# Two runs of high and low parts in the up products, and high parts first in the down units, of a hybrid encoder layer

## The chip, the cores and the metric

The kernel runs on one core of a Trainium2 chip. The metric is device time in microseconds of one execution, the median of several runs. Times of single instructions come from one profiled execution.

## What is computed

One encoder layer for 512 tokens of width 2048: a projection into a convolution group and an attention group, an output projection with a residual, and then a gated MLP with a width-3 convolution between its up-projection and its activation. The change is in the MLP:

```python
xn = rms_norm(x, ffn_norm_g[l])
up = jnp.einsum("bsd,df->bsf", xn, w_up[l])          # 2048 -> 2 x 5632
up = depthwise_conv(up, ffn_dw_w[l], ffn_dw_b[l])
gate, val = jnp.split(up, 2, axis=-1)
x = x + jnp.einsum("bsf,fd->bsd", jax.nn.silu(gate) * val, w_down[l])
return rms_norm(x, final_norm_g)
```

All inputs and outputs are float32.

## The kernel before, in words

**High and low parts.** Every product runs in the type float32r on TensorE. To keep float32's accuracy, each operand is split: its high part is a float32r copy that ScalarE makes (`whi`, L117), its low part the difference, which VectorE makes (`wlo`, L121). Of the four partial products three are kept: high by high, high by low, low by high (`mm3`, L128 to L136).

**The weights.** `plan` lists, in the order of use, a function for every weight unit of 128 x 1024; `weights()` (L158) hands out the next one and has made the three behind it by then (`AHEAD` is 3). A unit comes in by a DMA on SyncE's queue into one of seven raw buffers, and is split by `parts` (L114) into rings of four high and four low buffers (`NW` is 4). A buffer is written again when the unit four places back is no longer read.

**The up products.** The hidden width is done in 44 tiles f of 128, in chunks of four (`CH` is 4). In each f the gate tile and the value tile, each 2048 by 512 tokens, come from seven smaller products instead of eight, by Strassen's scheme in Winograd's form: seven sums of the weights' quarters (`factors`, L687) times seven sums of the activations' quarters (`comb`, made once at L652). Of each product c there are eight blocks. The activation block `comb[c][k]` holds its high part for 256 columns and its low part for the next 256, so one *wide* matmul of 512 columns with the weight's high part (L773) gives high by high in the left half of a bank and high by low in the right half. A *narrow* matmul of 256 columns (L779) with the weight's low part adds low by high into the right half. ScalarE and VectorE read both halves afterwards, add them, and combine the seven results (L814 to L846).

`up` (L764) does the products in pairs (0, 1), (2, 3), (4, 5), and 6 by itself. In a pair: eight wides of the first, one wide of the second, eight narrows of the first, eight narrows of the second, seven wides of the second. Product 6: seven wides, eight narrows, one wide. The tiles f = 0 and f = 3 go through `up_apart`, with 256 columns only.

**The banks.** `product_bank` (L754) gives the PSUM bank. From the second chunk on products 0 to 5 take turns in the three `mm` banks, and product 6 has the one bank `po`. The two `tr` banks belong to the down units there.

**The down units.** While chunk c is made, chunk c - 1 is multiplied into the output: behind products 3 and 6 of every f stands one down unit (`down_units`, L732; in the last chunk fewer). `down` (L915) takes one weight unit for two output tiles d; for each it does `mm3` over the four hidden tiles k: high by high, high by low, low by high, four times over, 12 wide matmuls in one `tr` bank. ScalarE copies the bank out (L926), and GpSimd's queue adds it to the sum in DRAM (L927). With `wide=True` the same function does the last units at the end, in `mm` and `tr` banks.

**The order.** A scheduler places every engine's instructions from the program's order and the buffers' dependences; within a queue all go in order. Before the change it put some matmuls of a down unit between the products in two f of most chunks. The function `tick` issues side work (statistics of the norm) behind a product; it has none left in the stretch that the change touches.

Of the kernel before, what the change touches and what calls it, by code (L numbers as in the profile page):

```python
# [10 lines left out]
F32 = mybir.dt.float32  # L11
# [5 lines left out]
P = 128  # L17
D = 2048
S = 512
# [15 lines left out]
U = 8  # L35
# [7 lines left out]
CH = 4  # L43
# [23 lines left out]
def layer(ctx: ExitStack, tc: tile.TileContext, xT, xG, xw, w_a, w_in, w_v, w_out, w_up, w_down, par, tab, g3, out, last_out):  # L67
    nc = tc.nc
# [5 lines left out]
    psm = ctx.enter_context(tc.tile_pool(name="psm", bufs=3, space=bass.MemoryType.PSUM))  # L74
    psa = ctx.enter_context(tc.tile_pool(name="psa", bufs=1, space=bass.MemoryType.PSUM))
# [9 lines left out]
    def t2(name, dt=F32):  # L85
        return tp.tile([P, S], dt, tag="t2k", name=name)
# [41 lines left out]
    def mm3(ps, w, wk, mh, ml, start, stop):  # L128
        hi, lo = w[:2]
        a = slice(wk * P, (wk + 1) * P)  # L130
        m = nc.tensor.matmul(ps, hi[:, a], mh, start=start, stop=False)  # L131
        if turned:
            turned.pop()
            pin(m)
        nc.tensor.matmul(ps, hi[:, a], ml, start=False, stop=False)  # L135
        return nc.tensor.matmul(ps, lo[:, a], mh, start=False, stop=stop)  # L136
# [4 lines left out]
    def tick(behind, mid=False):  # L141

        for todo in (steps, asteps):
            while todo and mid == (todo is asteps and amid[0]):
                try:
                    with tc.issue_after(behind.ins):
                        at = next(todo[0])
                    if todo is asteps:
                        amid[0] = at == "mid"
                    break  # L150
                except StopIteration:
                    todo.pop(0)
# [3 lines left out]
    plan, made = [], []  # L156

    def weights():  # L158
        at = weights.at
        weights.at += 1  # L160
        while len(made) < min(at + 1 + AHEAD, len(plan)):
            made.append(plan[len(made)]())
        return made[at]
# [78 lines left out]
    ps = psa.tile([P, 2, S], F32, tag="sc", name="idle")  # L242
# [3 lines left out]
    for k in range(KD):  # L246
        if k < CH:
            raw = t4([P, U * P], "raw")
            n = S + 2 * P + (0 if k else KD)
# [3 lines left out]
        else:  # L253
            if k % CH == 0:
                raw = t4([P, U * P], "raw")
            if k % CH == 0 or k == CH + 2:
                o, n = 2 * (k % CH) * P, 2 * (2 if k < 2 * CH else CH) * P
# [22 lines left out]
    for step in ORDER:  # L280
# [5 lines left out]
        i = next(a_ if step == "a" else q_)  # L286
# [280 lines left out]
    p, n = -1, 0  # L567
# [186 lines left out]
    def product_bank(f, c):  # L754

        n = 7 * f + c
        at = n % 6 if f < CH else 3 * (c == 6)
        if at < 3:
            return psm.tile([P, S], F32, tag="mm", name="pu")
        if at == 3:  # L760
            return psa.tile([P, S], F32, tag="po", name="pu")
        return psa.tile([P, S], F32, tag="tr", name="pu", bufs=2)

    def up(f, between):  # L764

        opened = {}

        def bank(c):
            return product_bank(f, c)

        def wides(c, w, ps, ks, stop=False):
            for k in ks:
                i = nc.tensor.matmul(ps, w[0][:, k * P:(k + 1) * P], comb[c][k], start=k == 0,  # L773
                                     stop=stop and k == ks[-1])
            return i

        def lows(c, w, ps, stop=False):
            for k in range(U):
                i = nc.tensor.matmul(ps[:, H:], w[1][:, k * P:(k + 1) * P], comb[c][k][:, :H], start=False,  # L779
                                     stop=stop and k == U - 1)  # L780
            return i

        def product(c):

            w = weights()
            if c == 6:
                ps = bank(c)
                wides(c, w, ps, range(U - 1))
                lows(c, w, ps)
                i = wides(c, w, ps, range(U - 1, U), stop=True)  # L790
            elif c % 2:
                ps = opened.pop(c)
                lows(c, w, ps)
                i = wides(c, w, ps, range(1, U), stop=True)
            else:
                ps, opened[c + 1] = bank(c), bank(c + 1)
                wides(c, w, ps, range(U))
                wides(c + 1, made[weights.at], opened[c + 1], range(1))
                i = lows(c, w, ps, stop=True)
            tick(i)  # L800
            between(c)
            return ps[:, :H], ps[:, H:]

        def copy(to, ps):
            nc.scalar.activation(to, ps, AF.Copy)  # L805

        def pair(name):
            return t2(name).rearrange("p (i t) -> p i t", i=2)

        def both(x):  # L810
            return x.unsqueeze(1).broadcast_to([P, 2, H])


        vv, low = pair("vv"), pair("pl")  # L814
        for i in range(2):
            m, l = product(i)
            copy(vv[:, i], m)
            copy(low[:, i], l)
        m7, l = product(2)
        add(vv, vv, low)  # L820
        low = pair("pl")
        copy(low[:, 0], l)
        m1, l = product(3)
        copy(low[:, 1], l)
        uu, v = pair("uu"), pair("vl")
        u, u2 = uu[:, 0], uu[:, 1]
        add(u2, m7, low[:, 0])
        add(v, vv, both(u2))
        m6, l = product(4)
        add(u, m1, low[:, 1])  # L830
        low = pair("pl")
        copy(low[:, 0], l)
        add(u2, u, m6)
        m2, l = product(5)
        add(u2, u2, low[:, 0])
        add(v, v, both(u2))
        add(vv[:, 1], vv[:, 1], u2)
        low, g = pair("pl"), pair("g")
        copy(low[:, 0], l)
        add(g[:, 0], u, m2)  # L840
        m3, l = product(6)
        copy(low[:, 1], l)
        add(g[:, 1], vv[:, 1], m3)
        add(g, g, low)
        g, v = (t.rearrange("p i t -> p (i t)") for t in (g, v))
        return g, v  # L846

    def up_apart(f, between):

        def begin(c):  # L850
            return weights(), product_bank(f, c)[:, :H]
# [46 lines left out]
    def hidden(f, between):  # L898
        return gated_tile(f, *(up_apart if f == CH - 1 else up)(f, between))
# [9 lines left out]
    def in_two(g):  # L909
        h, l = t2("hh", F32R), t2("hl", F32R)  # L910
        nc.scalar.activation(h, g, AF.Copy)
        nc.vector.tensor_sub(l, g, h.bitcast(F32))  # L912
        return h, l

    def down(hs, ds, wide=False):  # L915

        for d0 in ds:
            w = weights()
            for d in range(d0, d0 + U // CH):

                ps = (psm.tile([P, S], F32, tag="mm", name="pd") if wide and d % 5 > 1 else
                      psa.tile([P, S], F32, tag="tr", name="pd", bufs=2))
                for k in range(CH):
                    mm3(ps, w, (d - d0) * CH + k, *hs[k], k == 0, k == CH - 1)
                t = t2("pdc")
                nc.scalar.activation(t, ps, AF.Copy)  # L926
                nc.gpsimd.dma_start(xd[d], t, accum_op=ALU.add)  # L927
# [3 lines left out]
    def behind(c, i, at):  # L931
        if c == NCH - 1 and (i, at) == (0, 3):
            pend[-1] = in_two(pend[-1])
        down(pend, down_units(c, i, at))
# [6 lines left out]
    for c in range(NCH):  # L941
        hs = []
        for i in range(CH):
# [5 lines left out]
            if c and i == CH - 1:  # L949
                hs = [in_two(h) for h in hs]  # L950
            hs.append(hidden(c * CH + i, lambda at: None if last else meanwhile(c, i, at)))
        if c != NCH - 2:
            hs = [h if isinstance(h, tuple) else in_two(h) for h in hs]
# [4 lines left out]
    n = CH  # L958
# [17 lines left out]
    for d in down_units(NCH - 1, CH - 1, 6):  # L976
        down(pend, (d,), wide=True)
        last_weights(len(ws))
        last_weights(len(ws))
# [26 lines left out]
    for d in range(KD):  # L1006
        ps = psm.tile([P, S], F32, tag="mm", name="pd")[:, fm]
        for k in range(n):
            mm3(ps, ws[d // CH * CH + k], d % CH, hs[k][0][:, fm], hs[k][1][:, fm], k == 0, k == n - 1)
        i = nc.vector.tensor_add(x2[d][:, fm], x2[d][:, fm], ps)  # L1010
# [7 lines left out]
    wide = psa.tile([P, 2, S], F32, tag="sc", name="pt")  # L1018
    banks = [psa.tile([P, S], F32, tag="tr", name="pt", bufs=2) if g % 2 else wide[:, g // 2] for g in range(CH)]
    rb, xg = [], []  # L1020
    sums, v, r, y, w = (sm.tile([P, CH], F32, tag="rs" + c, name="rs" + c) for c in "lvryw")
    v, r, y, w = (t[:, :1] for t in (v, r, y, w))
# [12 lines left out]
    for g, ps in enumerate(banks):  # L1035
# [5 lines left out]
        for k in range(n):  # L1041
# [3 lines left out]
            i = nc.tensor.matmul(ps, hh[:, tm], dh, start=False, stop=False)  # L1045
# [104 lines left out]
```

## Time and profile before

| | |
|---|---|
| median of 3 runs | 2016.16 us (2015.9 to 2017.13) |
| the profiled execution | 2016.15 us |
| its span, first to last instruction | 2014.4 us |
| granted clock of TensorE, mean | 0.998 |
| up products, and the down units between them | 661.7 to 1937.3 us of the span |
| VectorE busy in that stretch | 1086.41 us |
| ScalarE busy in that stretch | 711.35 us |
| DMA in that stretch | 142 GB/s, engines busy for 0.60 of the time |

A profile line of a group has the source line, the engine, the operation, output and inputs with their shapes, the count, then busy time and mean duration in ns, then the idle time of the engine ahead of it and what ended that. A timeline line has the start and the duration in us; neighbours of one kind are merged (x9), and a bracket tells how long the engine stood idle and who released it. PE is TensorE's matmuls, PEld its weight loads, DVE is VectorE, ACT is ScalarE, POOL is GpSimd, SP is SyncE.

### The profile page before, as it was taken

The page shows a single profiled execution, that of the slowest core. Times are in us where ns is not written, and L with a number is a line of the kernel's source. Part 1 is how long each engine was busy: PE and PEld are TensorE (multiplying, and loading weights), DVE is VectorE, ACT ScalarE, POOL GpSimd, SP SyncE. Part 2 cuts the span into 40 slices and gives each one's busy share as a digit, 9 for nine tenths or more (in the row PEclk, how much of TensorE's full clock was granted, in tenths as well). Part 3 has the DMA queues.
Part 4 walks back from the last instruction along what each step waited for, and adds up shares of the span by engine and source line. Part 5 has one row for each costly group of instructions (what it writes and reads, how often), then busy time and mean ns, then how long its engine had stood idle before and what let it go on. Part 6 is the DMA issues. An engine that isn't in the chain of part 4 may idle for free.

```text
span 2014.4 us, 28027 instructions
## 1 busy us (share of the span) xinstructions
PE 2004.4 (100%) x10510; PEld 1715.7 (85%) x10510; DVE 1667.9 (83%) x2264; ACT 1054.7 (52%) x1689; POOL 169.4 (8%) x201
## 2 busy tenths in 40 slices
PE   9999999999999999999999999999999999999998
PEld 8888888888888998888888888888888888888887
DVE  7996888987576898887888888888888888889875
ACT  6323344476355665555555554555555555555563
POOL 0000000000002101111111111111111111110111
PEclk9999999999999999999999999999999999999999
DMA  7233333346348766556556556555565566564573
GB/s 258 84 106 93 113 95 107 105 139 211 100 136 213 189 163 152 139 129 152 133 135 148 131 131 154 132 139 141 127 145 145 127 145 147 131 141 128 145 206 129
DMA packets 98567, 284.25 MB, mean 141 GB/s; under 512 B 11008, under 2 KB 11520, under 8 KB 98432
## 3 DMA queue, kind: packets, MB, share of 16 engines
q1 hardware_dynamic: 71712, 231.07, 37.4%
q0 software_dynamic: 26720, 51.40, 17.1%
q8 instruction: 83, 1.36, 0.3%
q14 instruction: 52, 0.43, 0.1%
HBM read 227.90 MB, written 54.53 MB: 140 GB/s over the span
## 4 chain that ended last, share of the span: by engine, by line
PE 99%; DMA 0%; ACT 0%; DVE 0%; ACTq 0%; issue 0%; DVEq 0%
PE pu L773 27%; PE pu L779 14%; PE pd L136 8%; PE pd L131 8%; PE pd L135 8%; PE pj L131 6%; PE pj L135 6%; PE pj L136 6%; PE po L131 3%; PE po L135 3%; PE po L136 3%; PE pv L342 1%; PE pv L341 1%; PE pv L340 1%; PE po L535 1%; PE trp L518 1%
## 5 line engine op out<-in xcount | busy, mean ns | idle before, releaser
L117 ACT ACTIVATE whi<-raw 128x1024 fp32r<-128x1024 f32 x364 | 384.5, 1058 | 480.4 <-PE pj L135 131.7
L121 DVE TENSOR_TENSOR wlo<-raw,whi 128x1024 fp32r<-128x1024 f32 x364 | 444.5, 1222 | 208.5 <-ACT whi L117 198.0
L773 PE MATMUL pu<-xc,whi 128*128 128x512 f32 x2352 | 580.0, 391 | 0.0
L773 PEld LDWEIGHTS pu<-xc,whi 128*128 128x128 f32 x2352 | 433.5, 188 | 83.0
L779 PEld LDWEIGHTS pu<-xc,wlo 128*128 128x128 f32 x2352 | 306.8, 191 | 14.6
L779 PE MATMUL pu<-xc,wlo 128*128 128x256 f32 x2352 | 311.3, 283 | 0.0
L136 PE MATMUL pd<-hh,wlo 128*128 128x512 f32 x640 | 250.3, 391 | 0.0
L131 PE MATMUL pd<-hh,whi 128*128 128x512 f32 x640 | 249.7, 390 | 0.0
L135 PE MATMUL pd<-hl,whi 128*128 128x512 f32 x640 | 249.1, 390 | 0.0
L927 POOL DMA_DIRECT2D x2d<-pdc x160 | 138.9, 870 | 1099.0 <-ACT pdc L926 870.1
L131 PE MATMUL pj<-xh,whi 128*128 128x512 f32 x512 | 198.3, 392 | 0.1
L136 PE MATMUL pj<-xh,wlo 128*128 128x512 f32 x512 | 198.2, 390 | 0.0
L135 PE MATMUL pj<-xl,whi 128*128 128x512 f32 x512 | 198.2, 390 | 0.0
L805 ACT ACTIVATE pl<-pu 128x256 f32<-128x256 f32 x294 | 109.9, 382 | 150.1 <-PE pu L773 142.8
L117 ACT ACTIVATE whi<-ws 128x1024 fp32r<-128x1024 f32 x132 | 139.7, 1058 | 72.6 <-PE pu L773 54.2
L396 DVE SCALAR_TENSOR_TENSOR y<-ch,prm,y 128x501 f32<-128x501 f32 (+14 forms) x240 | 173.5, 740 | 4.4
L121 DVE TENSOR_TENSOR wlo<-ws,whi 128x1024 fp32r<-128x1024 f32 x132 | 161.2, 1221 | 14.8 <-ACT whi L117 14.8
L136 PEld LDWEIGHTS pd<-hh,wlo 128*128 128x128 f32 x640 | 120.1, 188 | 28.5 <-DVE wlo L121 3.3
L135 PEld LDWEIGHTS pd<-hl,whi 128*128 128x128 f32 x640 | 120.2, 188 | 25.0 <-DVE hl L912 0.4
L131 PEld LDWEIGHTS pd<-hh,whi 128*128 128x128 f32 x640 | 120.4, 188 | 22.6
L926 ACT ACTIVATE pdc<-pd 128x512 f32<-128x512 f32 x160 | 93.8, 588 | 79.1 <-PE pd L136 66.0
L131 PEld LDWEIGHTS pj<-xh,whi 128*128 128x128 f32 x512 | 96.0, 188 | 20.7 <-ACT g L276 0.3
(228 smaller groups left out, 2721.1 us busy)
## 6 DMA issues: line engine op xcount, KB each, us to landing
raw<-in_w_up SPq DMA_DIRECT2D x176, 512.0 KB, 3.9
raw<-in_w_down SPq DMA_DIRECT2D x88, 512.0 KB, 4.0
x2d<-pdc POOLq DMA_DIRECT2D x160, 256.0 KB, 4.8
raw<-in_w_in SPq DMA_DIRECT2D x60, 512.0 KB, 3.7
raw<-in_w_out SPq DMA_DIRECT2D x32, 512.0 KB, 3.6
raw<-in_w_v SPq DMA_DIRECT2D x16, 512.0 KB, 4.2
tab<-in_tab SPq DMA_DIRECT2D x32, 256.0 KB, 4.9
x<-in_xT SPq DMA_DIRECT2D x16, 256.0 KB, 6.1
```

Of the source, the lines that this page charges most:

```text
L117: i = nc.scalar.activation(hi[:, :n], raw[:, :n], AF.Copy)
L121: j = nc.vector.tensor_sub(lo[:, :n], raw[:, :n], hi[:, :n].bitcast(F32))
L131: m = nc.tensor.matmul(ps, hi[:, a], mh, start=start, stop=False)
L135: nc.tensor.matmul(ps, hi[:, a], ml, start=False, stop=False)
L136: return nc.tensor.matmul(ps, lo[:, a], mh, start=False, stop=stop)
L340: nc.tensor.matmul(ps, xh, wh[:, f], start=kk == 0, stop=False)
L396: nc.vector.scalar_tensor_tensor(y[:, a:b], h[:, a + j - PAD:b + j - PAD], prm[:, o + j:o + j + 1], y[:, a:b], op0=ALU.mult, op1=ALU.add)
L773: i = nc.tensor.matmul(ps, w[0][:, k * P:(k + 1) * P], comb[c][k], start=k == 0, stop=stop and k == ks[-1])
L779: i = nc.tensor.matmul(ps[:, H:], w[1][:, k * P:(k + 1) * P], comb[c][k][:, :H], start=False, stop=stop and k == U - 1)
L805: nc.scalar.activation(to, ps, AF.Copy)
L926: nc.scalar.activation(t, ps, AF.Copy)
L927: nc.gpsimd.dma_start(xd[d], t, accum_op=ALU.add)
```

## The change

From the second chunk on (f of 4 or more), `up` has two runs in place of the pairs: products 0 to 3, then 4 to 6. At the first product of a run, the banks of all of the run are taken, and the wides of all are issued (of the last product only the first); then come the narrows of each product in turn, and behind the narrows of the last one its other seven wides. So a run of four is 25 wides, 32 narrows, 7 wides; a run of three is 17 wides, 24 narrows, 7 wides. The wides of a run use weight units that `weights()` has already made, up to three ahead. For this, `product_bank` gives product 3 the bank `po` as well, which product 6 has; products 0, 1, 2, 4, 5 take turns in the three `mm` banks.

A down unit that isn't `wide` takes both its banks first, then for both output tiles the eight matmuls with the weight's high part (16 in all), then for each tile the four with the low part, its copy and its accumulating DMA. The number of matmuls, copies and DMAs is the same. The first chunk and the units at the end are as before.

```diff
     def product_bank(f, c):
         n = 7 * f + c
-        at = n % 6 if f < CH else 3 * (c == 6)
+        at = n % 6 if f < CH else 3 * (c % 3 == 0 and c > 0)
...
     def up(f, between):
         opened = {}
+        runs = ((0, 1), (2, 3), (4, 5), (6,)) if f < CH else ((0, 1, 2, 3), (4, 5, 6))
...
         def product(c):
             w = weights()
-            if c == 6:
+            run = next(r for r in runs if c in r)
+            if len(run) == 1:
                 ps = bank(c)
                 wides(c, w, ps, range(U - 1))
                 lows(c, w, ps)
                 i = wides(c, w, ps, range(U - 1, U), stop=True)
-            elif c % 2:
+            elif c == run[-1]:
                 ps = opened.pop(c)
                 lows(c, w, ps)
                 i = wides(c, w, ps, range(1, U), stop=True)
             else:
-                ps, opened[c + 1] = bank(c), bank(c + 1)
-                wides(c, w, ps, range(U))
-                wides(c + 1, made[weights.at], opened[c + 1], range(1))
+                if c == run[0]:
+                    for j in run:
+                        opened[j] = bank(j)
+                        wides(j, w if j == c else made[weights.at + j - c - 1], opened[j],
+                              range(1 if j == run[-1] else U))
+                ps = opened.pop(c)
                 i = lows(c, w, ps, stop=True)
...
     def down(hs, ds, wide=False):
+        def bank(d):
+            return (psm.tile([P, S], F32, tag="mm", name="pd") if wide and d % 5 > 1 else
+                    psa.tile([P, S], F32, tag="tr", name="pd", bufs=2))
         for d0 in ds:
             w = weights()
-            for d in range(d0, d0 + U // CH):
-                ps = (psm.tile([P, S], F32, tag="mm", name="pd") if wide and d % 5 > 1 else
-                      psa.tile([P, S], F32, tag="tr", name="pd", bufs=2))
+            two = range(d0, d0 + U // CH)
+            banks = [] if wide else [bank(d) for d in two]
+            for ps, d in zip(banks, two):
                 for k in range(CH):
-                    mm3(ps, w, (d - d0) * CH + k, *hs[k], k == 0, k == CH - 1)
+                    a = slice(((d - d0) * CH + k) * P, ((d - d0) * CH + k + 1) * P)
+                    for i, x in enumerate(hs[k]):
+                        nc.tensor.matmul(ps, w[0][:, a], x, start=k + i == 0, stop=False)
+            for d in two:
+                if wide:
+                    ps = bank(d)
+                    for k in range(CH):
+                        mm3(ps, w, (d - d0) * CH + k, *hs[k], k == 0, k == CH - 1)
+                else:
+                    ps = banks[d - d0]
+                    for k in range(CH):
+                        a = slice(((d - d0) * CH + k) * P, ((d - d0) * CH + k + 1) * P)
+                        nc.tensor.matmul(ps, w[1][:, a], hs[k][0], start=False, stop=k == CH - 1)
                 t = t2("pdc")
                 nc.scalar.activation(t, ps, AF.Copy)
                 nc.gpsimd.dma_start(xd[d], t, accum_op=ALU.add)
```

## The prediction, made before the changed kernel was run

> **What bounds the kernel now.** I read the page first: busy time, granted clock, the chain that ended last.
>
> ```profile
> span 2014.4 us, 28027 instructions
> ...
> PE 2004.4 (100%) x10510; PEld 1715.7 (85%) x10510; DVE 1667.9 (83%) x2264; ACT 1054.7 (52%) x1689; POOL 169.4 (8%) x201
> ...
> PE 99%; DMA 0%; ACT 0%; DVE 0%; ACTq 0%; issue 0%; DVEq 0%
> ...
> L117 ACT ACTIVATE whi<-raw 128x1024 fp32r<-128x1024 f32 x364 | 384.5, 1058 | 480.4 <-PE pj L135 131.7
> ...
> L805 ACT ACTIVATE pl<-pu 128x256 f32<-128x256 f32 x294 | 109.9, 382 | 150.1 <-PE pu L773 142.8
> ```
>
> TensorE is busy for 2004.4 of 2014.4 us, and 99% of the chain is TensorE. The change removes no matmul. So the only time to be had in the gated-MLP stretch is what its matmuls lose against their own steady pitch, and the first question is how much that is. I take it from the stretch between the first and the last up product (windows view, then the groups by shape inside it, then the timeline of one f, TensorE alone).
>
> ```profile
> 661.70:1937.30 1275.60, 1275.60 (x6868) 1105.38 (x6867) 1086.41 (x1383) 711.35 (x1104) 138.00 (x159) 1.00 0.60 142
> ```
>
> ```profile
> L779 PE MATMUL pu<-xc,wlo 128*128 128x256 f32 x2352 | 311.3, 283 | 0.0
> ...
> L135 PE MATMUL pu<-xc,whi 128*128 128x256 f32 x112 | 31.7, 283 | 0.0
> L136 PE MATMUL pu<-xc,wlo 128*128 128x256 f32 x112 | 31.7, 283 | 0.0
> L131 PE MATMUL pu<-xc,whi 128*128 128x256 f32 x112 | 31.7, 283 | 0.0
> ```
>
> ```profile
> 1198.03 2.20 PE L773 MATMUL pu<-xc,whi 128*128 128x512 f32 x9
> 1200.07 2.08 PE L779 MATMUL pu<-xc,wlo 128*128 128x256 f32 x16
> 1201.99 3.59 PE L773 MATMUL pu<-xc,whi 128*128 128x512 f32 x15
> 1205.41 1.12 PE L779 MATMUL pu<-xc,wlo 128*128 128x256 f32 x8
> 1206.37 0.40 PE L131 MATMUL pd<-hh,whi 128*128 128x512 f32 x1
> 1206.60 0.40 PE L135 MATMUL pd<-hl,whi 128*128 128x512 f32 x1
> 1206.84 0.39 PE L131 MATMUL pd<-hh,whi 128*128 128x512 f32 x1
> 1207.16 0.50 PE L136 MATMUL pd<-hh,wlo 128*128 128x512 f32 x1
> 1207.50 0.40 PE L131 MATMUL pd<-hh,whi 128*128 128x512 f32 x1
> ...
> 1209.14 0.39 PE L773 MATMUL pu<-xc,whi 128*128 128x512 f32 x1
> 1209.36 1.11 PE L779 MATMUL pu<-xc,wlo 128*128 128x256 f32 x8
> 1210.31 1.78 PE L773 MATMUL pu<-xc,whi 128*128 128x512 f32 x7
> 1211.93 0.39 PE L135 MATMUL pd<-hl,whi 128*128 128x512 f32 x1
> ...
> 1214.87 2.20 PE L773 MATMUL pu<-xc,whi 128*128 128x512 f32 x9
> 1216.91 2.08 PE L779 MATMUL pu<-xc,wlo 128*128 128x256 f32 x16
> 1218.83 3.36 PE L773 MATMUL pu<-xc,whi 128*128 128x512 f32 x14
> 1222.03 1.12 PE L779 MATMUL pu<-xc,wlo 128*128 128x256 f32 x8
> ```
>
> Matmuls overlap, so their cost is the distance between starts, not the duration. A wide one (512 columns) costs (1200.07 - 1198.03)/9 = 0.2267 us, a narrow one (256) (1201.99 - 1200.07)/16 = 0.120 us. The stretch holds 2352 + 3 x 112 = 2688 narrow ones and 6868 - 2688 = 4180 wide ones: 4180 x 0.2267 + 2688 x 0.120 = 947.6 + 322.6 = 1270.2 us. It lasts 1275.6. So **5.4 us in all** are lost, and no re-ordering can win more than about that (0.27%), unless it changes the pitch itself. Two losses can be seen in the rows, and the change touches both.
>
> **The change part by part.**
>
> *Waits in the down unit.* At 1206.84 to 1207.50 two wide pitches are 0.32 and 0.34 us: 0.66 against 2 x 0.2267 = 0.453, so 0.21 us lost. The waits view of the weight loader names the cause and the count, and VectorE's timeline the time:
>
> ```profile
> PEld pd L136 <- DVE wlo L121: 3.3, 9, 0.4
> ```
>
> ```profile
> 1205.28 0.69 DVE L906 TENSOR_TENSOR uy<-uy 128x512 f32<-128x512 f32 x1
> 1205.88 1.22 DVE L121 TENSOR_TENSOR wlo<-raw,whi 128x1024 fp32r<-128x1024 f32 x1
> ...
> 1213.23 1.23 DVE L121 TENSOR_TENSOR wlo<-ws,whi 128x1024 fp32r<-128x1024 f32 x1 [0.38 <-ACT whi L117]
> 1214.37 0.42 DVE L827 TENSOR_TENSOR uu<-pu,pl 128x256 f32<-128x256 f32 x1
> 1215.99 1.23 DVE L121 TENSOR_TENSOR wlo<-raw,whi 128x1024 fp32r<-128x1024 f32 x1 [1.20 <-ACT whi L117]
> 1217.13 0.69 DVE L828 TENSOR_TENSOR vl<-vv,uu 128x512 f32<-128x512 f32 x1
> 1217.73 0.42 DVE L830 TENSOR_TENSOR uu<-pu,pl 128x256 f32<-128x256 f32 x1
> 1218.14 1.23 DVE L121 TENSOR_TENSOR wlo<-raw,whi 128x1024 fp32r<-128x1024 f32 x1
> ```
>
> The unit's low part ends at 1205.88 + 1.22 = 1207.10, and its first user wants to start at about 1207.07 with its weights already loaded. This happens nine times, once a chunk, in the last f, where VectorE also splits three gated tiles: 9 x 0.21 = 1.9 us. After the change the unit takes 16 wides first (3.63 us), and it stands behind four whole products instead of three: it starts 25 x 0.2267 + 32 x 0.120 + 7 x 0.2267 = 11.1 us into the f instead of 1206.37 - 1198.03 = 8.3. Its first low part is wanted at 1198.03 + 14.7 = 1212.8, 5.7 us behind 1207.10. I take the whole **1.9 us** as gained; between 0, if VectorE's new order makes the low part that much later, and 1.9.
>
> *Wides behind narrows.* Wides that follow wides keep 0.2267. Those that follow narrows do not: 15 took 1205.41 - 1201.99 = 3.42 (15 x 0.2267 = 3.40), 14 took 3.20 (3.174), 7 took 1.62 (1.587): 0.02 to 0.033 us over, and more wides do not add to it, so it is paid once for each stretch of narrows, not per matmul. What is left of the 5.4 us says the same: 5.4 - 1.9 = 3.5. In TensorE's program order I count 189 stretches of narrows before (f 4 to 43: four each, one more in two f of nine chunks, and 11 in the first chunk) and 91 after (two each, and the same 11): 3.5/189 = 0.019 us each. I take 0.020, nearest to the count, and 98 x 0.020 = **2.0 us** gained; the bounds are 0, if it is not the switch that costs, and 98 x 0.033 = 3.2.
>
> [...]
>
> *What is wanted earlier.* A run of four wants its high parts within 25 wides. Within an f, product 1 is wanted where it was (after 8 wides, 1.81 us). Product 2 came after 16 wides and 16 narrows (5.55 us) and comes after 16 wides (3.63); product 3 likewise moves from 7.36 to 5.44, or further where it stood inside the down unit; product 6 from 5.55 to 3.63 us behind the first down unit; its low part from 7.1 to 5.8. Products 4 and 5, and all other low parts, are wanted when they were, or later. ScalarE's timeline shows how far ahead the copies of products 2, 3 and 6 of this f are:
>
> ```profile
> 1192.77 1.06 ACT L117 ACTIVATE whi<-raw 128x1024 fp32r<-128x1024 f32 x1 [1.44 <-PE pu L773]
> ...
> 1198.01 1.06 ACT L117 ACTIVATE whi<-raw 128x1024 fp32r<-128x1024 f32 x1 [1.90 <-PE pd L135]
> ...
> 1212.13 1.07 ACT L117 ACTIVATE whi<-ws 128x1024 fp32r<-128x1024 f32 x1 [3.57 <-PE pu L773]
> ```
>
> They end at 1193.8, 1199.1 and 1213.2, and the new order wants them at 1198.03 + 3.6 = 1201.7, + 5.4 = 1203.5 and + 20.2 = 1218.2: 7.9, 4.4 and 5.0 us ahead. The low part of product 6 ends at 1213.23 + 1.23 = 1214.5 and is wanted at 22.3, so at 1220.3. The ring of four high parts is used up by one run; the buffer for product 3 is the one of the down unit before, and is free 8 lows (1.81 us) before the f starts, 7.2 us before it is wanted, against a copy of 1.06. Cost 0, covered by these leads; if a lead is gone, each us late costs 40 us, once an f.
>
> *Banks and evictions.* Four products now end within 4.5 us and are read by six copies of 0.382 us, 2.3 us of ScalarE. Products 4 and 5 take the banks of 0 and 1, which end 6.6 and 7.6 us into the f and are wanted at 16.5: nothing waits, and where the last chunk has no down unit between, they are still wanted 4.5 us later. A down unit holds both its banks from the start; their last copies are from a unit 11 us back or more. The two results of a unit leave 0.9 us apart instead of 2.7, for ScalarE, then GpSimd's queue, with the same number of DMAs; SyncE's loads move with the raw buffers that the low parts free, and land with the same leads. Cost 0 for all of it; a gain is excluded, since TensorE waited for none of these.
>
> *The sum.* The profiled execution took 2016.15 us, 1.75 more than its span, and the median shown is 2016.16, the same. 2016.15 - 1.9 - 2.0 = **2012.3 us**, a span of 2010.5; 0.19% less.
>
> **The rivals.**
> 1. *The switch costs nothing*, and the 3.5 us belong to something that the order doesn't touch (the rounding of the two pitches alone moves that sum by about 1 us). Against: the three stretches, all over, and in proportion to no count of wides. Only the waits go: 2016.15 - 1.9 = 2014.3. [...]
> 2. *The switch costs what the single stretches show*: 98 x 0.033 = 3.2, with the waits 5.1: 2011.0. For it: the 7 wides at 1210.31. Against: 189 x 0.033 = 6.2 would be more than was lost.
> 3. *Slower: the bank that products 3 and 6 share.* Before, only product 6 used it; now product 6 can't open until VectorE has read product 3, and in VectorE's new order that read stands behind the low part of the second down unit, which needs the first one's buffer, free only at that unit's end. So: unit's end, a low part (1217.13 - 1215.99 = 1.14), two adds that read product 3 and its neighbour (0.41 and 0.42): 1.97 us, against 16 wides = 3.63 until product 6 opens. It decides from 1.66 us more on VectorE at that place. One more low part ahead of it (1.14) still costs nothing; two (2.28) cost 0.6 us, in each of the 36 f with two down units: 22 us, 2034, and 0.22 us an f is enough to be slower by 0.2%. Against: VectorE is 85% busy here (1086 of 1275.6) and has 0.38 and 1.20 us of idle time at just these places above.
> 4. *It doesn't do what it says*: a wait returns behind the new highs. The order as built shows the two runs in every f from 4 on and the highs first in every narrow down unit, so only a late buffer could do this; 1 to 2 us of waits, about 2014.
>
> **How the numbers follow.** Forecast 0.60, over 2011.6 to 2013.2; rival 1 0.14, rival 2 0.12, rival 3 0.08, rival 4 0.06. A measurement of this kernel tells 0.2% from no change, 4.0 us: below 2012.1 is faster, above 2020.2 slower. Faster: rival 2 and two fifths of the forecast, 0.12 + 0.24 = 0.36. Slower: most of rival 3, 0.06. Within: 0.58. For 8 in 10 the range leaves out rival 3 and the far ends: 2010.8 to 2014.4.
>
> **What would show it.** The loader's wait for the low part in the down unit is gone; the same stretch lasts 1271.7 us; behind 32 or 24 narrows the 7 wides again take about 1.62 us, not more, and narrows stay at 0.120; TensorE shows no new wait at product 6's first high. A stretch of 1273.7 with those waits gone is rival 1. A wait for VectorE at product 6 is rival 3. It is wrong altogether if 32 narrows in a row run slower than 0.120, or if the leads of ScalarE's copies, 4.4 us at the least, are eaten by its new order.

## The result, and the profile after

| | before | after |
|---|---|---|
| median, with its runs on the same chips | 2016.77 us (14 runs, 2015.90 to 2017.85) | 2012.70 us (14 runs, 2011.88 to 2013.73) |
| profiled execution | 2016.15 us | 2013.73 us |
| its span | 2014.4 us | 2011.8 us |
| first up matmul's start to the last one's start | 1275.22 us | 1272.78 us |

The ratio is 0.998, with an interval of 0.9973 to 0.9986: the changed kernel is faster by 0.14 to 0.27%. The forecast was 2012.3. The profiled execution of the changed kernel is the slowest of its 14, by 1.0 us over their median, and one place below accounts for that much.

In the changed kernel L774 are the wide up matmuls, L780 the narrow ones, L934 the down unit's high parts and L944 its low parts. The page of the changed kernel:

```profile
span 2011.8 us, 28094 instructions
...
PE 2001.2 (99%) x10510; PEld 1716.8 (85%) x10510; DVE 1659.2 (82%) x2264; ACT 1065.7 (53%) x1689; POOL 171.1 (9%) x201
...
PE 97%; DMA 1%; DVE 0%; ACT 0%; issue 0%; ACTq 0%; POOL 0%; POOLq 0%; DVEq 0%; SPq 0%
```

The work is the same (10510 matmuls, 2264 operations on VectorE), and TensorE is still the chain. The windows view over the up stretch, as for before (start and end, length, then busy time and count of PE, PEld, DVE, ACT, POOL, granted clock, DMA share, GB/s):

```profile
661.80:1934.90 1273.10, 1272.26 (x6868) 1106.54 (x6868) 1076.77 (x1381) 722.21 (x1104) 139.67 (x159) 1.00 0.58 142
```

The same 6868 matmuls at the same clock take 1273.1 us where they took 1275.6; TensorE idles for 0.84 of them. Now the loader's waits, the view that gave the first term. The columns after the arrow are total us, times, longest:

```profile
PEld st L194 <- DVE nl L190: 0.9, 1, 0.9
...
PEld pu L774 <- issue: 0.2, 1, 0.2
```

The line for the down unit's low part (3.3 us, nine times) is gone. New are `st <- nl` (with an `st <- nh` of 0.5 us beside it) and one small wait at an up product. TensorE's timeline of the f that the prediction read:

```profile
1198.04 5.83 PE L774 MATMUL pu<-xc,whi 128*128 128x512 f32 x25
1203.71 4.00 PE L780 MATMUL pu<-xc,wlo 128*128 128x256 f32 x32
1207.54 1.78 PE L774 MATMUL pu<-xc,whi 128*128 128x512 f32 x7
1209.16 0.39 PE L934 MATMUL pd<-hh,whi 128*128 128x512 f32 x1
...
1212.78 1.98 PE L944 MATMUL pd<-hh,wlo 128*128 128x512 f32 x8
1214.60 4.01 PE L774 MATMUL pu<-xc,whi 128*128 128x512 f32 x17
1218.45 3.04 PE L780 MATMUL pu<-xc,wlo 128*128 128x256 f32 x24
1221.32 1.78 PE L774 MATMUL pu<-xc,whi 128*128 128x512 f32 x7
```

Take the distances between starts: 25 wides 5.67 (25 x 0.2267 = 5.67), 32 narrows 3.83 (32 x 0.120 = 3.84), the 7 wides behind them 1.62 against 1.587, 16 wides of the down unit 3.62 (3.627), its 8 low parts 1.82 (1.814). Only the 7 wides behind the narrows lose, 0.033 us, as they did behind 8 narrows before. Narrows win back some 0.01 (3.83 for 3.84, and 24 in 2.87 for 2.88). These rows are rounded to 0.01 us; on the mean of all such places in the two traces the seven wides lose 0.027 us, behind 8, 16, 24 and 32 narrows alike, and the narrows win back about 0.006.

The new wait lies in the first chunk, which the change doesn't touch. VectorE, then TensorE, at 676 us of the changed kernel:

```profile
675.24 0.69 DVE L684 TENSOR_TENSOR acc<-acc,sq 128x512 f32<-128x512 f32 x1 [1.96 <-DMA sq<-sq]
...
676.98 0.68 DVE L190 TENSOR_TENSOR nl<-acc,nh 128x512 fp32r<-128x512 f32 x1
```

```profile
676.11 0.28 PE L136 MATMUL pu<-xc,wlo 128*128 128x256 f32 x1
676.65 0.49 PE L194 MATMUL st<-nh,ones 128*128 128x512 f32 x1 [0.26 <-ACT nh L189]
677.72 0.50 PE L194 MATMUL st<-nl,ones 128*128 128x512 f32 x1 [0.58 <-DVE nl L190]
```

The sum of squares for the norm comes back from DRAM; VectorE waits 1.96 us for it, and the two matmuls of the statistics, which stand in the middle of TensorE's queue, start 0.42 and 0.85 us late, and the next one 0.11: 1.38 us in all. In the profiled execution of before, the same addition ran at 673.10 with no wait. Of the ten traces of this study (before, after and eight experiments) five show such a stand, of 0.4 to 1.4 us, and five show none, though only one edit (of the statistics, below) touches the order of the first chunk. So it belongs to the execution, not to the change.

The account is then: 1275.22 - 1272.78 = 2.44 us shorter as profiled; without the 1.38 of the stand, **3.8 us**, where the prediction had 3.9. The medians are 4.07 apart.

### The profile page after: what moved, and what is told of

It reads as the page before. It is cut to its first block, busy times and chain, and to the rows that moved or that the text cites. A ratio compares the mean times of both kernels' runs of the same rounds, so it can differ in the third digit from the quotient of the medians.

```text
span 2011.8 us, 28094 instructions
## 1 busy us (share of the span) xinstructions
PE 2001.2 (99%) x10510; PEld 1716.8 (85%) x10510; DVE 1659.2 (82%) x2264; ACT 1065.7 (53%) x1689; POOL 171.1 (9%) x201
## 4 chain that ended last, share of the span: by engine, by line
PE 97%; DMA 1%; DVE 0%; ACT 0%; issue 0%; ACTq 0%; POOL 0%; POOLq 0%; DVEq 0%; SPq 0%
PE pu L774 27%; PE pu L780 14%; PE pd L934 14%; PE pd L944 7%; PE pj L131 6%; PE pj L135 6%; PE pj L136 6%; PE po L131 3%; PE po L135 3%; PE po L136 3%; PE pv L341 1%; PE pv L340 1%; PE pv L342 1%; PE pd L136 1%; PE pd L135 1%; PE pd L131 1%
## 5 line engine op out<-in xcount | busy, mean ns | idle before, releaser
L774 PE MATMUL pu<-xc,whi 128*128 128x512 f32 x2352 | 562.8, 390 | 0.0
L774 PEld LDWEIGHTS pu<-xc,whi 128*128 128x128 f32 x2352 | 435.9, 188 | 87.0 <-issue 0.2
L780 PEld LDWEIGHTS pu<-xc,wlo 128*128 128x128 f32 x2352 | 293.9, 192 | 6.8
L780 PE MATMUL pu<-xc,wlo 128*128 128x256 f32 x2352 | 296.1, 283 | 0.0
L934 PE MATMUL pd<-hl,whi 128*128 128x512 f32 x608 | 236.5, 389 | 0.0
L934 PE MATMUL pd<-hh,whi 128*128 128x512 f32 x608 | 236.5, 389 | 0.0
L944 PE MATMUL pd<-hh,wlo 128*128 128x512 f32 x608 | 150.1, 389 | 0.0
L934 PEld LDWEIGHTS pd<-hl,whi 128*128 128x128 f32 x608 | 114.1, 188 | 23.8 <-DVE hl L917 0.2
L944 PEld LDWEIGHTS pd<-hh,wlo 128*128 128x128 f32 x608 | 114.1, 188 | 23.7
L934 PEld LDWEIGHTS pd<-hh,whi 128*128 128x128 f32 x608 | 114.1, 188 | 23.6
L136 PEld LDWEIGHTS pj<-xh,wlo 128*128 128x128 f32 x512 | 96.1, 188 | 20.5
```

What stands on the lines that cost most here:

```text
L934: nc.tensor.matmul(ps, w[0][:, a], x, start=k + i == 0, stop=False)
L944: nc.tensor.matmul(ps, w[1][:, a], hs[k][0], start=False, stop=k == CH - 1)
```

## The experiments

All are variants of the changed kernel unless the text says otherwise. "Stretch" means from the first up matmul's start to the last one's start.

**Each part of the change alone.** The first keeps the runs and puts the old `down` back:

```diff
-            banks = [] if wide else [bank(d) for d in two]
-            for ps, d in zip(banks, two):
-                ...
+            for d in range(d0, d0 + U // CH):
+                ...
+                    mm3(ps, w, (d - d0) * CH + k, *hs[k], k == 0, k == CH - 1)
```

> The two runs of the up products as after, the down unit as before (high, high, low, per block). 92 stretches of narrows against 91 after and 189 before. Theory (each stretch costs 0.02 us, and the down unit's wait goes because the unit stands 2.8 us later in the f): both terms are won by the runs alone, 2012.7 to 2013, and the weight loader's wait for the low part in the down unit is gone. Rival (the wait goes because the unit takes its high parts first): the nine waits stay, 1.9 us more than after, 2014.6.

Measured: 2013.23 us (11 runs, 2012.31 to 2013.88), ratio 0.9982 (0.9973 to 0.999). The stretch is 1272.60 us with a stand of 0.97 at 676. TensorE's timeline at the same place:

```profile
1198.32 5.83 PE L774 MATMUL pu<-xc,whi 128*128 128x512 f32 x25
...
1209.43 0.39 PE L131 MATMUL pd<-hh,whi 128*128 128x512 f32 x1
1209.66 0.39 PE L135 MATMUL pd<-hl,whi 128*128 128x512 f32 x1
1209.88 0.39 PE L136 MATMUL pd<-hh,wlo 128*128 128x512 f32 x1
```

The low part is again the third matmul of the unit, and it doesn't wait: starts are 0.22 or 0.23 apart. The unit starts 1209.43 - 1198.32 = 11.1 us into the f, not 8.3, and these 2.8 us are enough for a low part that was some 0.2 us late. The runs alone give both terms, within 0.2 us of the expected 2012.7 to 2013.

The second keeps the pairs of before and takes only the new `down`, high parts first (the diff is the other half of the change).

> The down unit's high parts first as after, the up products in pairs as before; 189 stretches of narrows as before. Theory: the nine waits of 0.21 us go, the stretches stay: 2016.8 - 1.9 = 2014.9, and the up stretch lasts 1273.3 us. Rival (the waits were all of the gain, the stretches cost nothing): as after, 2012.7. Second rival (highs first moves the wait to the gated tiles' split, which the first eight wides now all need): 2016 to 2017.

Measured: 2027.27 us, ratio 1.0062 (1.0049 to 1.0076): slower, and the expectation missed by 12 us. The loader's waits:

```profile
PEld pu L773 <- issue: 16.8, 38, 2.7
PEld pu L773 <- ACT pl L805: 7.4, 18, 2.4
```

No wait for a low part in the down unit is left, so high parts first do remove it by themselves. But 56 waits at up products have come. VectorE and then TensorE, at one of them (L827 reads product 2 out of its bank, L830 product 3):

```profile
1220.52 1.23 DVE L121 TENSOR_TENSOR wlo<-raw,whi 128x1024 fp32r<-128x1024 f32 x1 [1.61 <-PE pd L939]
1221.67 0.42 DVE L827 TENSOR_TENSOR uu<-pu,pl 128x256 f32<-128x256 f32 x1
1222.00 0.41 DVE L830 TENSOR_TENSOR uu<-pu,pl 128x256 f32<-128x256 f32 x1
```

```profile
1220.27 2.43 PE L773 MATMUL pu<-xc,whi 128*128 128x512 f32 x9
1222.54 1.71 PE L779 MATMUL pu<-xc,wlo 128*128 128x256 f32 x13
```

Read the first bracket. All four buffers of low parts are full; the next low part may be written when the down unit's last low matmul has ended, and now all eight of those stand at the unit's end. So VectorE stood idle for 1.61 us, and the reads of products 2 and 3 stood behind it. Product 5 opens the bank of product 2 with its first wide, the ninth here: the nine took 2.27 us, not 2.04, 0.23 late. That is the mechanism of rival 3, on another bank. Two of the six runs, the profiled one among them, took over 2034 us, the other four 2026.0 to 2027.5. The profiled one lost some 8.2 us at once, in the last chunk, about what sets it apart from the median:

```profile
1861.04 2.98 PE L773 MATMUL pu<-xc,whi 128*128 128x512 f32 x8 [1.95 <-ACT pl L805]
...
1866.63 3.62 PE L779 MATMUL pu<-xc,wlo 128*128 128x256 f32 x16
1870.05 3.26 PE L773 MATMUL pu<-xc,whi 128*128 128x512 f32 x9
```

VectorE had waited 3.51 us for a weight's DMA there, TensorE stood twice, and 16 narrows took 3.42 us, 0.214 each instead of 0.120: see the last section.

To test the bank as the cause, the third gives product 5 a bank that nothing else uses there:

```diff
         at = n % 6 if f < CH else 3 * (c == 6)
+        if f >= CH and c == 5:
+            return psa.tile([P, 2, S], F32, tag="sc", name="pu")[:, 0]
```

> e2_down_only (pairs, and the down unit's high parts first; 2027.3) with a bank of its own for product 5 from the second chunk on, so that it need not wait for the read of product 2. In the trace of e2_down_only product 5 starts 0.23 us late behind most second-half down units: VectorE's queue holds the low part of the next down unit ahead of that read, and this low part waits until the unit before gives its buffer back, now at its very end. Theory: those waits, about 35 x 0.23 = 8 us, go: 2019; the rest of its loss, in the last chunk behind a late load, stays. Rival (the loss is in ScalarE's copies or the gated tiles, whichever bank): 2027.

Measured: 2019.51 us, ratio 1.0018 (1.001 to 1.0027): 7.8 us better than the one above, as expected. In its trace the 38 waits `pu <- issue` are gone. So the bank is shown as the cause of most of the loss. Three of the 11 runs took 4 to 6 us more than the median; they have no trace, so the cause is open. What is left over the kernel before (in the trace, 18 waits for ScalarE's copies, of up to 1.5 us, and three for the gated tiles just behind the first chunk) wasn't pursued.

**The number of stretches of narrows.** With the new `down` kept, every product is done by itself, so that there are 290 stretches instead of 91:

```diff
-        runs = ((0, 1), (2, 3), (4, 5), (6,)) if f < CH else ((0, 1, 2, 3), (4, 5, 6))
+        runs = ((0, 1), (2, 3), (4, 5), (6,)) if f < CH else tuple((c,) for c in range(7))
```

> As after, but every product by itself: seven wides, eight narrows, one wide; 290 stretches of narrows against 91. Theory (paid once a stretch): 199 x 0.02 = 4.0 us more than after, 2016.7, and 0.025 to 0.03 us in the wides behind each stretch. Rival (switches cost nothing): 2012.7.

Measured: 2016.31 us, ratio 0.9999 (0.999 to 1.0007), as expected. The loader has no wait in this stretch beside the stand at 676 us. TensorE's timeline, with the one wide of product 3 that stands behind its eight narrows, and the down unit:

```profile
1210.52 0.40 PE L774 MATMUL pu<-xc,whi 128*128 128x512 f32 x1
...
1213.27 0.39 PE L934 MATMUL pd<-hl,whi 128*128 128x512 f32 x1
...
1214.40 1.98 PE L944 MATMUL pd<-hh,wlo 128*128 128x512 f32 x8
```

The first twelve wides behind the narrows (1210.52 to 1213.27) take 2.75 us against 2.72, and the next five (1213.27 to 1214.40) 1.13, the steady pitch: the cost is paid in the first wides, then it is over. In three kernels, each without its stand and its waits:

| | stretches of narrows | stretch, us |
|---|---|---|
| after | 91 | 1271.14 |
| before | 189 | 1273.36 |
| every product alone | 290 | 1275.11 |

From the first to the last it is 3.97/199 = 0.020 us for each stretch of narrows, which the forecast had. The two halves give 0.023 and 0.017.

Does the cost hang on the stretch or on every change of width? The next one alternates wide and narrow in each product, which makes 2250 stretches of one narrow:

```diff
+                    for k in range(U):
+                        wides(c, w, ps, range(k, k + 1))
+                        i = nc.tensor.matmul(ps[:, H:], w[1][:, k * P:(k + 1) * P], comb[c][k][:, :H], ...)
```

> As e3_singles, but within a product a wide and a narrow in turn, eight times; 2250 stretches of narrows, all but a few of one matmul. If each switch costs 0.02 us: 2159 x 0.02 = 43 us more than after, 2056. If the cost lies in the first five wides behind a stretch (pitches of 234, 236, 228, 232 and 231 ns against 227 in the trace of before) and the first narrow gets 7 ns back (113 against 120), a single wide costs 7 and the narrow returns 7: about as after, 2012 to 2014. Rival (switches cost nothing): 2012.7.

Measured: 2027.44 us, ratio 1.0054 (1.0041 to 1.0067), between the two expectations: both missed. The stretch is 1286.26 us: 15.1 more than after's 1271.14 for 2159 more stretches, 0.007 us each. TensorE's timeline:

```profile
1202.60 0.40 PE L774 MATMUL pu<-xc,whi 128*128 128x512 f32 x1
1202.85 0.28 PE L797 MATMUL pu<-xc,wlo 128*128 128x256 f32 x1
1202.96 0.40 PE L774 MATMUL pu<-xc,whi 128*128 128x512 f32 x1
...
1206.14 0.40 PE L774 MATMUL pu<-xc,whi 128*128 128x512 f32 x1
```

Ten pairs take 3.54, 0.354 each against 0.347: on the mean of the whole trace a wide between two narrows takes 0.236 us and a narrow between two wides 0.117. So a narrow and a wide in turn cost a third of a stretch of eight, and the price is not a fixed one per change of width. The same trace tells what it hangs on: at the 76 places where a down unit's wides follow, the seven wides behind a single narrow lose 0.030 us on the mean (1213.20 to 1214.84 at one of them: 1.64, in rows of 0.01), about the 0.027 that they lose behind 8 to 32. So the number of wides that follow counts, not that of the narrows.

**The stand at 676 us.** The changed kernel, with the statistics' matmuls one product later:

```diff
-        rstd2.append((yield from factor(acc2, D, "rstd2", rest=2, free=True)))
+        rstd2.append((yield from factor(acc2, D, "rstd2", rest=3, free=True)))
```

> After, with the second norm's column sums multiplied one product later (rest=3 for 2). In the profiled execution of after TensorE stood 1.4 us there, for sums that come back from DRAM; in that of before it did not, though both have the same order up to that place. Theory (the arrival of the sums differs from run to run, and explains most of the 1.9 us between the fastest and the slowest run of after): 2011.5, and the runs lie closer. Rival (the spread is from elsewhere): 2012.7 and the same spread.

Measured: 2012.74 us (11 runs, 2012.42 to 2013.57), ratio 0.998 (0.9971 to 0.9989): missed, no better than after's 2012.70. The runs lie closer (1.15 us from end to end, 1.85 in after), but there are fewer of them. VectorE in its trace:

```profile
673.32 0.69 DVE L684 TENSOR_TENSOR acc<-acc,sq 128x512 f32<-128x512 f32 x1
```

The sums came in time in this execution, as in before, so the trace doesn't test the edit. Its stretch, without the stand, is 1271.45 us, which is after's 1272.78 less 1.38 but for 0.05. The median says that the stand is not in the typical run of after, or that the edit doesn't remove it; which, stays open. No version here beats after.

**How near rival 3 was.** Two kernels put work on VectorE ahead of the read of product 3, once and twice, with TensorE's order pinned to that of after. The extra operation is added work whose result nothing reads; in the second kernel the loop runs twice:

```diff
-        add(u, m1, low[:, 1])
+        if CH <= f < NF - CH:
+            x = made[weights.at + 2][1].bitcast(F32)
+            for _ in range(1):
+                y = psa.tile([P, 2, S], F32, tag="sc", name="more").rearrange("p i t -> p (i t)")
+                pin(add(y, x, x))
+            pin(add(u, m1, low[:, 1]))
...
```

> After, with one sum of 1024 columns put on VectorE between the second down unit's low part and the read of product 3 (chunks 1 to 9), and TensorE's order of the runs held as written. Ahead of the read then stand the sum (1.14) and an add that the scheduler takes first (0.60): 1.74 us against the 1.66 that the prediction gave as the point from which the shared bank decides. Theory: 0.1 to 0.3 us in each of 36 f, 3 to 11 us: 2016 to 2024, with TensorE waiting for VectorE at product 6's first high part. Rival (VectorE's idle time, 15% of the stretch, takes it up): 2012.7.

> As e7_one_more with two such sums: 2.28 + 0.60 = 2.88 us ahead of the read, 1.2 us past the point: 36 x 1.2 = 44 us, 2057. Rival (idle time takes it up): 2012.7 to 2020.

Measured: 2033.47 us, ratio 1.0082 (1.0068 to 1.0096), and 2074.67 us, ratio 1.0286 (1.027 to 1.0301). Both are dearer than expected (2016 to 2024, and 2057). First after, with nothing added: VectorE at the place in question (L835 reads product 3; left out is L832, which reads product 2).

```profile
1214.85 1.23 DVE L121 TENSOR_TENSOR wlo<-raw,whi 128x1024 fp32r<-128x1024 f32 x1 [1.50 <-PE pd L944]
...
1216.33 0.41 DVE L835 TENSOR_TENSOR uu<-pu,pl 128x256 f32<-128x256 f32 x1
1216.66 0.68 DVE L833 TENSOR_TENSOR vl<-vv,uu 128x512 f32<-128x512 f32 x1
```

Then the kernel with one operation more, VectorE and TensorE (L837 and L844 are what L833 and L835 are in after, L843 is the added one):

```profile
1222.73 1.23 DVE L121 TENSOR_TENSOR wlo<-raw,whi 128x1024 fp32r<-128x1024 f32 x1 [1.50 <-PE pd L955]
...
1224.20 1.23 DVE L843 TENSOR_TENSOR more<-wlo 128x1024 f32<-128x1024 f32 x1
1225.34 0.69 DVE L837 TENSOR_TENSOR vl<-vv,uu 128x512 f32<-128x512 f32 x1
1225.94 0.42 DVE L844 TENSOR_TENSOR uu<-pu,pl 128x256 f32<-128x256 f32 x1
```

```profile
1222.47 3.79 PE L774 MATMUL pu<-xc,whi 128*128 128x512 f32 x16
1226.50 0.47 PE L774 MATMUL pu<-xc,whi 128*128 128x512 f32 x1 [0.25 <-DVE uu L844]
1226.81 3.04 PE L782 MATMUL pu<-xc,wlo 128*128 128x256 f32 x24
```

And TensorE with two more:

```profile
1209.55 3.79 PE L774 MATMUL pu<-xc,whi 128*128 128x512 f32 x16
1214.71 0.47 PE L774 MATMUL pu<-xc,whi 128*128 128x512 f32 x1 [1.38 <-DVE uu L844]
```

Product 6 should open 16 x 0.2267 = 3.63 us behind product 4's start. With one more it opens at 4.03, 0.40 late; with two at 5.16, 1.53 late. Ahead of the read stand, as the expectations counted, the added operation (1.14 between starts) and also L833, which in after stands behind it (0.60), 1.74 us in all; with two, 2.88. The slack is 1.74 - 0.40 = 1.34 or 2.88 - 1.53 = 1.35 us, the same from both. After's own rows give it too: the read ends at 1216.33 + 0.41 = 1216.74, 2.14 behind product 4's start at 1214.60, and the bank is free 0.14 later (in the kernel with one more the read ends at 1226.36 and the matmul starts at 1226.50): 3.63 - 2.28 = 1.35. The lone wide adds 0.08 each time (0.31 to the next start, not 0.23). So 36 x 0.48 = 17.3, and 2.1 more in the first such f, where VectorE has two more operations ahead of the read, are 19.4 of the 20.8 us that the median rose above after's; for two, 36 x 1.61 = 58.0, and 2.2, of 62.0.

## Why the prediction was right, step by step

- **What bounds it, and 5.4 us to be had.** Held: TensorE is the chain in both, no matmul went, and the gain is below the bound.
- **Waits in the down unit, 1.9 us.** Held in size: nine waits (1.86 us by the pitches) are gone. The prediction named two reasons, 16 wides first and a later start. Either is enough, as the two halves of the change show; in this kernel the high parts first bring nothing measurable beside the runs (2013.23 without, 2012.70 with, intervals all but equal), and beside the pairs they cost 10 us.
- **Wides behind narrows, 0.020 us for each of 98.** Held: 0.020 from 199 more stretches. Between before and after alone it is 0.023, 2.2 us for the term of 2.0; that the new waits below take 0.26 of it back, so that the sum fits, is chance. Rival 1, that the switch costs nothing, is out: in both traces seven wides behind narrows take 1.614 us and seven among wides 1.587, so the spacing doesn't follow from the width alone here. Rival 2 took a single row's 0.033 for the whole price. It is too much because that row is rounded and because the narrows give about 0.006 back, which the prediction hadn't seen.
- **What is wanted earlier, cost 0.** Held: the loader's waits have no line for a copy of ScalarE at an up product. So rival 4, a wait behind the new highs, is out too.
- **Banks and evictions, cost 0.** Held but for 0.23 us, and 0.03 more for a gated tile. In the last chunk some f have no down unit between the two runs, so product 6's first wide follows product 3 closely. In one of them the scheduler put that wide behind four narrows, and it still waits for the shared bank. TensorE of the changed kernel, and the read of product 3 on VectorE:

```profile
1849.78 0.63 PE L780 MATMUL pu<-xc,wlo 128*128 128x256 f32 x4
1850.38 0.47 PE L774 MATMUL pu<-xc,whi 128*128 128x512 f32 x1
```

```profile
1849.81 0.42 DVE L835 TENSOR_TENSOR uu<-pu,pl 128x256 f32<-128x256 f32 x1
```

  The four narrows should take 0.48 and the wide starts 0.60 behind them, when the read has ended (1850.23); it and the next matmul lose 0.20 together, and another such place 0.03.

- **Rival 3, slower by the shared bank, 0.08.** It didn't happen, but it was nearer than the prediction said. The mechanism is right, and the second half of the change alone runs into it on another bank. The point was put at 1.66 us and is 1.35: the chain was counted from the next product's first start (1214.60), but the low part starts 0.25 later (1214.85), 0.09 behind the end of the unit's last matmul (1212.78 + 1.98 = 1214.76), and the matmul starts 0.14 behind the read's end; the two adds take 0.08 less than was counted. "One more low part ahead of it (1.14) still costs nothing" stands by this slack, though no run tries it, with 0.2 us to spare, not 0.5. The argument against it, that VectorE has idle time at these places, was no argument: that idle time (1.50 us in the bracket) is the wait for the buffer itself, ahead of everything that stands behind it.
- **What the prediction left out.** The stand at 676 us, which moves a single execution by up to 1.4 us, a third of the whole effect. Set against the profiled execution alone, the gain would have looked like 2.4.

## What to carry to other kernels

When an engine is busy for 99% of the span, subtract its steady pitches from the stretch before weighing any re-ordering: the rest bounds the gain, and its rows say in which kind of place it sits. Grouping matmuls of one width was worth some 0.02 us here for each group saved, however long the groups were (8 to 32); it pays only as long as the banks it holds come free in time: with product 6 opened 0.40 us late in the f shown, the kernel took 20.8 us more than after. Idle time of an engine counts as cover only for work that isn't queued behind the very wait that makes it idle: VectorE's 1.50 us covered none of the operation added behind it.

## What the runs showed of the hardware

- A stretch of narrow matmuls costs 0.020 us whether it has 8, 16, 24 or 32 of them, and 0.007 when narrows and wides take turns one by one. The first five wides behind it pay (233, 236, 228, 232 and 231 ns against 227, means of the traces), and the first narrow comes early (113 to 114 against 120). Why, the runs don't tell.
- A stand of TensorE of 1.95 us was followed by half its granted clock. In the kernel with the new `down` alone, TensorE stood from 1859.1 to 1861.0 (1.95 us) and again from 1864.0 to 1866.1 (2.05). The windows view of that kernel; the granted clock is the third number from the end:

```profile
1858.90:1861.00 2.10, 0.20 (x1) 0.00 (x0) 2.10 (x4) 1.19 (x4) 0.00 (x0) 1.00 0.01 4
...
1861.80:1863.60 1.80, 1.80 (x6) 1.18 (x5) 1.80 (x3) 0.98 (x3) 0.00 (x0) 0.56 0.00 0
...
1866.00:1872.00 6.00, 5.93 (x22) 5.48 (x23) 6.00 (x8) 2.62 (x5) 0.00 (x0) 0.50 0.75 203
```

  The clock was 1.00 before the first stand and in the first 0.8 us behind it, 0.56 on the mean of the next 1.8 us, and 0.50 for the 6 us from the end of the second: 22 matmuls. In the kernel with one operation more on VectorE, a stand of 2.37 us that ended at 764.3 us left the clock at 1.00 (762 to 770). In the one with two more, a stand of 3.6 us at the same place was followed by 0.68 on the mean of 766 to 770 us, by 0.93 from 770 to 776, and by 1.00 from 776 to 780. So the length of a single stand doesn't put the three in order: the clock fell behind 1.95 and 3.6 us, and not behind 2.37. What else enters stays open.
